# Attention of two heads at a time on the two halves of the PE array, with other PSUM banks

## The chip, the cores and the metric

One core of a Trainium2 chip runs the whole kernel. The metric is the device time of one execution in microseconds (us). Engines: PE is TensorE (matmuls), DVE is VectorE, ACT is ScalarE, POOL is GpSimd, SP issues the DMAs.

## What is computed

The reference runs one sequence of 256 tokens, 1024 features, in float32 through two blocks. The first block has two layers, each a mixer and a gated feed-forward with a short convolution. Each mixer has two attentions of 8 heads with 64 channels a head, so there are four attentions, which this case is about:

- even mixer, second half: chunked attention with a bias by relative position (relb);
- even mixer, first half: attention to 64 keys a query, chosen by index scores (4 index heads, relu, weighted sum, the 64 largest);
- odd mixer, second half: window attention of 8 query heads on 2 key heads, with a sink in the softmax;
- odd mixer, first half: causal attention with forget gates added to the logits.

```python
logits = einsum('bqhd,bshd->bhqs', q, k) * dh ** -0.5   # plus bias, mask, gates or sink
p = softmax(logits); out = einsum('bhqs,bshd->bqhd', p, v)
y = concatenate([first half, second half]); h = h + y @ w_out
```

The second block (a gated delta rule, a long convolution, a feed-forward, a gate) follows; the change does not touch it.

## The kernel before

Everything stays on the chip as [features, tokens] or [tokens, features] tiles; the weights (some 190 MB in pieces of 1 MB) are read once, in order, by SP. Matmuls with weights run in three products of parts: each piece is split into two parts `hi` (ScalarE, line 208) and `lo` (VectorE, line 209), each input `xs` likewise. Matmuls of the attention run in plain float32, which the profile shows as two passes each. A planner orders each engine's instructions before the run, by priority in the order of the program and by its own costs; on the chip each engine works through its own fixed queue. So PE's queue holds matmuls of projections (`mmA`, `mmB`) and of the output projection (`mmO`) between the steps of the softmax.

`attend` (lines 522 to 550) does one head. `at_s` are the logits in one PSUM bank of tag s: queries 0:128 against keys 0:128, queries 128:256 against keys 0:256, with 64 rows of the array (64 channels), head 0 of a pair on partitions 0 to 63, head 1 on 64 to 127. `logits` adds the mask or bias on VectorE into `at_l`; two reductions give minus the maxima `at_nm`; ScalarE takes exps into `at_p` with the sums `at_sm`; VectorE takes reciprocals and multiplies. Three transposes go into `at_t` (one bank, tag tr), ScalarE copies them to `at_pT`, and `at_y` (two matmuls with 64 columns of the array, so 64 partitions of the output) sums over keys. `attention` (552 to 560) runs eight heads, two in one bank of tag y, which is then split into `xs1` (lines 296 and 297).

PSUM has 8 banks. In a mixer (line 638) mm has 4, s 2, tr 1, y 1; the tag t of small products is put on s (line 642). `out_proj` (562 to 578) asks for four mm banks at once (`ac`), each for two feature tiles; its first two weight pieces belong to the half of the heads that came first and need no output of the attention in progress, the other two do; `residual` (line 372) adds each bank to `h`, and the feed-forward `ffn` starts from that `h` (its products are `mmU`). The weights' parts have two buffers each of `hi` and `lo` and one more from the phase's own pool (lines 162 to 173), taken in turn.

`to_feat` (596) transposes through bank s; the index scores (721 to 732), `fk` (845 to 850), `rel_logits` (743), `mask_logits` (615) and `forget_logits` (859) go head by head; `rel_logits` loads each head's bias into its own tile `relb`.

Of the kernel before, what the change touches and what calls it, by code (L numbers as in the profile page):

```python
# [19 lines left out]
T = 256  # L20
D = 1024
# [30 lines left out]
def weight_spec():  # L52
    """Pieces of the weight matrices (matrix, first k tile, k tiles, first column, columns), in order of use."""
# [42 lines left out]
def constants():  # L96
# [23 lines left out]
    # one level of a doubling: identity minus the lower (upper) left blocks, within 64 positions  # L120
# [31 lines left out]
class Weights:  # L152
    """Weight pieces in order: loaded whole, and split into two parts that add up to them exactly."""
# [60 lines left out]
def emit(ctx, tc, A):  # L214
# [7 lines left out]
    def phase(stack, name, tags):  # L222
        """PSUM banks of a phase: tag -> number."""
# [25 lines left out]
    # an early use of the scalar engine: its table is there when the data come  # L249
# [15 lines left out]
    def mmA(out, w, xs, m, k0=0, start=True, stop=True, ks=None):  # L265
        """out [128 features, T] += the piece's m-th 128 columns against xs, both in two parts."""
# [9 lines left out]
    def mmN(out, raw, x, m):  # L276
        """the same in float32."""
# [4 lines left out]
    def mmB(out, w, xs, j, c0=0, cn=None):  # L282
        """out [128 tokens of half j, columns] = xs^T against the piece."""
# [8 lines left out]
    def split_into(xs_k, src, scale=None):  # L292
        """xs_k [128, (k tiles,) 2T] = the two parts of src (times scale)."""
# [22 lines left out]
    def rsqrt(out, m, n):  # L316
        """out = 1/sqrt(m) of a small tile, by Newton's steps; few columns each on their own."""
# [16 lines left out]
    def square_acc(k, src, dst, **scale):  # L334
        """dst [128, T] = running sum over k of src's squares."""
# [8 lines left out]
    def mean_cols(*parts):  # L344
        """sums over features / D of [128, T] tiles, as columns [128 tokens, 2] in PSUM."""
# [6 lines left out]
    def row_bcast(col, name, ps=None):  # L352
        """columns [128 tokens, 2] -> [128, T] in PSUM, the same row on every partition."""
# [18 lines left out]
    def residual(i, ps):  # L372
        """h += ps [128, 2, T], two feature tiles; acc = the running sum of h's squares."""
# [14 lines left out]
    def pieces_A(name, xs, n, use, parts=None):  # L388
        """n pieces of a matrix with 8 k tiles; use(i, psum [128, 2, T])."""
# [14 lines left out]
    def ffn(up, dn, g, conv, beside=None):  # L404
        with ExitStack() as st:
# [5 lines left out]
            def scale(dst, ps):  # L411
                """dst = ps times the tokens' factors, two channel tiles."""
# [3 lines left out]
            # without a convolution the factors come after the product; else only the first pairs go ahead of them  # L416
# [77 lines left out]
    def pick_rows(p):  # L494
        """[128, 8] bf16: column n picks the rows n of the three parts of running sums."""
# [6 lines left out]
    def thrice(p, src, n, tag="thrice"):  # L502
        """[128, n, 128] of [128, n, 8]: three copies for the three parts' rows, zero elsewhere."""
# [6 lines left out]
    def three_parts(g, p, ps, tag="rest"):  # L510
        """g = bf16 parts of [128, w] in PSUM that add up to it: the first in rows 0:64, the others in 64:96 and 96:128."""
# [8 lines left out]
    QB = ((0, 128), (128, 384))  # columns of the two query blocks: keys 0:128, keys 0:256  # L520

    def attend(hd, qT, kT, v, logits, ap, y, sink):
        """One head: qT, kT [64, T]; v(kb) [128, 64]; y [64, T] in PSUM."""
        ps = bank("s", "at_s")
        mm(ps[:, 0:128], qT[:, 0:128], kT[:, 0:128])
        mm(ps[:, 128:384], qT[:, 128:256], kT)
        L = logits(hd, ps)
        nm = small(2, "at_nm", 3)
        for j, (a, b) in enumerate(QB):
            V.tensor_reduce(nm[:, j:j + 1], L[:, a:b], AX.X, OP.max, negate=True)  # L530
        if sink is not None:
            V.tensor_scalar(nm, nm, sink[1][:, hd:hd + 1], None, OP.min)
        pr = ap.tile([128, 384], F32, tag="at_p", name="at_p", bufs=3)
        sm = small(2, "at_sm", 3)
        for j, (a, b) in enumerate(QB):
            S.activation(pr[:, a:b], L[:, a:b], AF.Exp, bias=nm[:, j:j + 1], accum_out=sm[:, j:j + 1])
        if sink is not None:
            es = small(2, "at_es", 3)
            S.activation(es, nm, AF.Exp, bias=sink[0][:, hd:hd + 1])
            V.tensor_tensor(sm, sm, es, OP.add)  # L540
        V.reciprocal(sm, sm)
        for j, (a, b) in enumerate(QB):
            V.tensor_scalar(pr[:, a:b], pr[:, a:b], sm[:, j:j + 1], None, OP.mult)
        tp = bank("tr", "at_t")
        for b in range(3):
            transpose(tp[:, 128 * b:128 * b + 128], pr[:, 128 * b:128 * b + 128])
        pT = ap.tile([128, 384], F32, tag="at_pT", name="at_pT", bufs=3)
        S.copy(pT, tp[:, :384])
        mm(y, v(0), pT[:, 0:256], True, False)
        mm(y[:, 128:256], v(1), pT[:, 256:384], False, True)  # L550

    def attention(qT, kT, vN, logits, ap, ys, k0, kv=lambda hd: hd, sink=None):
        """Eight heads; qT: [128, pairs, T] (head hd on partitions 64*(hd%2)), vN [128, 2, 64*heads]."""
        for p in range(4):
            yp = bank("y", "at_y")
            for hd in (2 * p, 2 * p + 1):
                o, c = 64 * (hd % 2), kv(hd)
                attend(hd, qT[o:o + 64, p], kT(hd, o), lambda kb: vN[:, kb, 64 * c:64 * c + 64], logits, ap,
                       yp[o:o + 64, :T], sink)
            split_into(ys[:, k0 + p], yp[:, :T])  # L560

    def out_proj(name, ys, first):
        """h += ys against a matrix; the half of the k tiles from `first` on comes first."""
# [16 lines left out]
    def rope(dst, src, nh, ap):  # L580
        """src, dst [128, 2, nh*64]."""
# [14 lines left out]
    def to_feat(dst, src, n):  # L596
        """src [128 tokens, 2, n*128] -> dst [128, n, T]."""
        for a in range(0, n, 2):
            ps = bank("s", "tf")
# [6 lines left out]
    def nat(name, xs, *parts):  # L606
        """A piece by the stationary tokens; parts: (destination [128, 2, ..], its column, piece's column, n, scale)."""
# [7 lines left out]
    def mask_logits(m, ap):  # L615
        def f(hd, ps):
            t = ap.tile([128, 384], F32, tag="at_l", name="at_l", bufs=3)
            V.tensor_tensor(t, ps[:, :384], m, OP.add)
            return t
        return f  # L620

    def log1pexp(dst, x, n):
        """dst = log(1 + exp(-|x|)), by the series of atanh."""
# [14 lines left out]
    ATT = {"mm": 4, "s": 2, "tr": 1, "y": 1}  # L638

    def att_phase(st, name):  # L640
        phase(st, name, ATT)
        banks["t"] = banks["s"]

# [1 line left out]
    with ExitStack() as st:  # L645
# [6 lines left out]
        # index keys and weights, index queries: in float32  # L652
# [9 lines left out]
        # the tensor engine's clock rises with work: it starts before the data come  # L662
        warm = bank("s", "warm")
# [30 lines left out]
        # layer norm of the index keys  # L694
# [852 lines left out]
```

## Time and profile before

| | |
|---|---|
| time, median of 3 runs | 1282.49 us (1282.23 to 1282.65) |
| span of the profiled execution | 1280.9 us, first to last instruction |
| mean granted TensorE clock in it | 0.990 |
| PE, DVE, ACT, POOL busy | 98%, 76%, 56%, 1% |
| four attentions, by PE's first at_s to last at_y | 62.7 to 91, 118.4 to 144, 375.7 to 404, 426.9 to 453 us |

The profile gives no time for the profiled execution other than its span; the median of the runs is 1.6 us above it. Busy time of PE counts a matmul from its start to its modelled end, and matmuls overlap, so what a matmul costs in a stream is read from start to start. A form such as 64*128 is rows times columns of the array in use.

### The profile page before, as it was taken

Reading aid. Unit: us, or ns where it says so; the run is one execution under the profiler, and the core shown is the slowest. Engines: PE = TensorE matmul, PEld = TensorE weight load, DVE = VectorE, ACT = ScalarE, POOL = GpSimd, SP = SyncE. Lnnn points to the kernel's source line nnn. Section 1 sums busy time; section 2 is a strip of 40 time slices with the busy share of each in tenths; the row PEclk is TensorE's granted clock in tenths of the full one; section 3 lists DMA queues with packets and bytes.
Section 4 is the critical chain, followed back from the end, with each engine's and each line's share of the span. In section 5 each row is a group of like instructions: output and inputs, shape, how many; then the busy total and the mean of one; then the engine's idle time right before and its main releaser. Section 6 shows DMA issues by size and latency. Waiting matters only on the chain.

```text
span 1280.9 us, 25239 instructions
## 1 busy us (share of the span) xinstructions
PE 1252.6 (98%) x10452; PEld 1192.3 (93%) x10452; DVE 976.9 (76%) x2024; ACT 717.7 (56%) x1204; POOL 11.6 (1%) x21
## 2 busy tenths in 40 slices
PE   8999999999999999999999999999999999999997
PEld 8978899999988889999988998889899999999997
DVE  6976698785497679878549888889997778666546
ACT  4465566664365556565425379888643654444433
POOL 0000000000000000000010000000000000000000
PEclk8999999999999999999999999999999999999999
DMA  6543355555342255554514332212234556555542
GB/s 228 181 153 132 132 180 186 195 179 187 135 165 88 78 198 182 184 195 170 193 64 177 133 132 100 100 35 78 88 133 147 182 193 205 190 194 189 181 154 86
DMA packets 29923, 195.45 MB, mean 153 GB/s; under 512 B 3568, under 2 KB 5104, under 8 KB 9712
## 3 DMA queue, kind: packets, MB, share of 16 engines
q1 hardware_dynamic: 29808, 193.83, 42.8%
q8 instruction: 82, 1.34, 0.4%
q14 instruction: 33, 0.27, 0.1%
HBM read 192.77 MB, written 1.05 MB: 151 GB/s over the span
## 4 chain that ended last, share of the span: by engine, by line
PE 74%; issue 11%; ACT 3%; DVE 3%; POOL 1%; ACTq 0%; POOLq 0%; DVEq 0%
PE mmU L260 29%; PE mmD L260 15%; PE mmA L260 12%; PE mmB L260 4%; PE mmO L260 3%; PE mmF L260 2%; PE at_y L260 2%; PE at_s L260 1%; PE sr L260 1%; ACT hi L208 1%; PE do L260 1%; PE at_t L263 1%; DVE lo L209 1%; PE mc L260 0%; ACT xbd L1150 0%
## 5 line engine op out<-in xcount | busy, mean ns | idle before, releaser
L208 ACT CAST hi<-raw 128x1024 fp32r<-128x1024 f32 (+2 forms) x273 | 336.3, 1252 | 322.4 <-PE mmU L260 138.6
L209 DVE TENSOR_TENSOR lo<-raw,hi 128x1024 fp32r<-128x1024 f32 (+2 forms) x273 | 400.1, 1476 | 134.5 <-ACT hi L208 133.9
L260 PE MATMUL mmU<-xs,hi 128*128 128x256 f32 x2112 | 373.6, 280 | 3.8 <-DVE h L385 3.8
L260 PEld LDWEIGHTS mmU<-xs,hi 128*128 128x128 f32 x2112 | 323.5, 188 | 4.4 <-ACT xs L299 3.2
L260 PE MATMUL mmU<-xs,lo 128*128 128x256 f32 x1056 | 296.4, 281 | 1.8 <-DVE lo L209 1.8
L260 PE MATMUL mmA<-xs,hi 128*128 128x256 f32 x1152 | 224.9, 291 | 0.2 <-ACT hi L208 0.2
L260 PEld LDWEIGHTS mmU<-xs,lo 128*128 128x128 f32 x1056 | 198.6, 188 | 2.5 <-DVE lo L209 2.4
L260 PE MATMUL mmD<-hid,hi 128*128 128x256 f32 x1056 | 190.2, 283 | 0.0
L260 PEld LDWEIGHTS mmA<-xs,hi 128*128 128x128 f32 x1152 | 181.8, 191 | 2.8 <-issue 1.5
L260 PE MATMUL mmA<-xs,lo 128*128 128x256 f32 x576 | 166.1, 289 | 1.3 <-DVE lo L209 1.2
L260 PEld LDWEIGHTS mmD<-hid,hi 128*128 128x128 f32 x1056 | 164.7, 192 | 0.0
L260 PE MATMUL mmD<-hid,lo 128*128 128x256 f32 x528 | 149.4, 283 | 0.0
L260 PEld LDWEIGHTS mmA<-xs,lo 128*128 128x128 f32 x576 | 110.0, 191 | 2.8 <-DVE lo L209 1.7
L1274 DVE SCALAR_TENSOR_TENSOR cv<-cpad,par,cv 128x256 f32<-128x256 f32 x240 | 107.6, 478 | 0.5
L260 PEld LDWEIGHTS mmD<-hid,lo 128*128 128x128 f32 x528 | 101.4, 192 | 0.0
L260 PE MATMUL mmB<-hi,xs 128*128 128x256 f32 x416 | 77.8, 285 | 0.9 <-DVE h L385 0.9
L260 PEld LDWEIGHTS mmB<-hi,xs 128*128 128x128 f32 x416 | 64.8, 190 | 2.2 <-issue 1.8
L260 PE MATMUL mmA<-hg,raw 128*128 128x256 f32 x256 | 65.1, 391 | 0.9 <-PE mmD L260 0.9
L452 DVE SCALAR_TENSOR_TENSOR cv<-mmU,par,cv 128x255 f32<-128x255 f32 (+1 forms) x144 | 60.9, 474 | 1.6 <-ACT cv L450 1.3
L260 PE MATMUL mmB<-lo,xs 128*128 128x256 f32 x208 | 59.4, 285 | 0.0
L260 PEld LDWEIGHTS mmA<-hg,raw 128*128 128x128 f32 x256 | 46.5, 193 | 6.3 <-PE mmD L260 1.1
L260 PE MATMUL mmO<-xs,hi 128*128 128x256 f32 x256 | 49.5, 288 | 0.0
(448 smaller groups left out, 1765.5 us busy)
## 6 DMA issues: line engine op xcount, KB each, us to landing
raw<-in_wts_dram SPq DMA_DIRECT2D x157, 1024.0 KB, 4.8
raw<-in_wts_dram SPq DMA_DIRECT2D x24, 896.0 KB, 4.5
relb<-in_relb_dram SPq DMA_DIRECT2D x8, 192.0 KB, 4.1
h<-in_xT_dram SPq DMA_DIRECT2D x4, 256.0 KB, 3.9
out_dram<-xg SPq DMA_DIRECT2D x2, 512.0 KB, 2.6
cst<-in_cst_dram SPq DMA_DIRECT2D x1, 640.0 KB, 8.8
buf<-in_g_plp_dram SPq DMA_DIRECT2D x1, 512.0 KB, 5.0
gfin<-in_g_fin_dram SPq DMA_DIRECT2D x1, 512.0 KB, 5.2
```

The lines of the kernel that those rows point to most:

```text
L208: self.nc.scalar.copy(hi[:, a:b], r[:, a:b])
L209: self.nc.vector.tensor_tensor(lo[:, a:b], r[:, a:b], hi[:, a:b].bitcast(F32), OP.subtract)
L260: PE.matmul(out, lhsT=lhsT, rhs=rhs, start=start, stop=stop, skip_group_check=True)
L263: PE.transpose(out, in_, ident)
L452: V.scalar_tensor_tensor(y[:, d:], x[:, :T - d], cw[:, 3 * ch + 2 - d:3 * ch + 3 - d], y[:, d:], OP.mult, OP.add)
L1274: V.scalar_tensor_tensor(cv[:, k], cpad[:, k, t:t + T], cw[:, t:t + 1], cv[:, k], OP.mult, OP.add)
```

## The change

Two heads take each step together. `attend` is gone; `attention` runs four times, once a pair. The logits of both heads go into one tile of two banks (`bank2`), the head on rows 0 to 63 and the head on rows 64 to 127 in turn, one bank each. Add, maxima, products and copy are single instructions for both heads; the exps stay one a head and query block. The probabilities stay in the logits' tile `at_l`. The products with v go in turn to the two column halves, which are two halves of the partitions of the same bank. The sink's exp takes one instruction for both heads and blocks, with an add ahead of it. PSUM is shared as mm 3, s 2, tr 2, y 1, so that s and tr hold one pair each, and t is put on y. Index scores, `fk`, masks, biases and forget gates go by pairs; `to_feat` uses s and tr in turn; the biases by relative position are loaded straight into `at_l`. `out_proj` is as it was. Comments are dropped.

```diff
+    def bank2(tag, name):
+        p, tag, n = banks[tag]
+        return p.tile([128, 2, 512], F32, tag=tag, name=name, bufs=n // 2)
...
     def attention(qT, kT, vN, logits, ap, ys, k0, kv=lambda hd: hd, sink=None):
+        two = (slice(0, 64), slice(64, 128))
         for p in range(4):
+            heads = (2 * p, 2 * p + 1)
+            ps = bank2("s", "at_s")
+            for first in (True, False):
+                for m, hd in enumerate(heads):
+                    q, k = qT[two[m], p], kT(hd, 64 * m)
+                    if first:
+                        mm(ps[:, m, 0:128], q[:, 0:128], k[:, 0:128])
+                    else:
+                        mm(ps[:, m, 128:384], q[:, 128:256], k)
+            L = logits(p, ps[:, :, :384])
+            nm, sm = small(4, "at_nm", 3), small(4, "at_sm", 3)
+            for j, (a, b) in enumerate(QB):
+                V.tensor_reduce(nm[:, 2 * j:2 * j + 2], L[:, :, a:b], AX.X, OP.max, negate=True)
...
+            pr = L
+            for m in range(2):
+                for j, (a, b) in enumerate(QB):
+                    c = slice(2 * j + m, 2 * j + m + 1)
+                    S.activation(pr[:, m, a:b], pr[:, m, a:b], AF.Exp, bias=nm[:, c], accum_out=sm[:, c])
+            if sink is not None:
+                es = small(4, "at_es", 3)
+                V.tensor_tensor(by_j(es), by_j(nm), both(sink[0]), OP.add)
+                S.activation(es, es, AF.Exp)
+                V.tensor_tensor(sm, sm, es, OP.add)
+            V.reciprocal(sm, sm)
+            for j, (a, b) in enumerate(QB):
+                V.tensor_tensor(pr[:, :, a:b], pr[:, :, a:b], sm[:, 2 * j:2 * j + 2].to_broadcast([128, 2, b - a]),
+                                OP.mult)
+            tp = bank2("tr", "at_t")
+            for m in range(2):
+                for b in range(3):
+                    transpose(tp[:, m, 128 * b:128 * b + 128], pr[:, m, 128 * b:128 * b + 128])
+            pT = ap.tile([128, 2, 384], F32, tag="at_pT", name="at_pT", bufs=2)
+            S.copy(pT, tp[:, :, :384])
             yp = bank("y", "at_y")
+            for kb in range(2):
+                for m, hd in enumerate(heads):
+                    c = 64 * kv(hd)
+                    mm(yp[two[m], 128 * kb:T], vN[:, kb, c:c + 64], pT[:, m, 256 * kb:256 + 128 * kb], kb == 0, kb == 1)
             split_into(ys[:, k0 + p], yp[:, :T])
...
     def to_feat(dst, src, n):
         for a in range(0, n, 2):
-            ps = bank("s", "tf")
+            ps = bank2("s" if a % 4 else "tr", "tf")[:, 0]
...
-            t = ap.tile([128, 384], F32, tag="at_l", name="at_l", bufs=3)
-            V.tensor_tensor(t, ps[:, :384], m, OP.add)
+            t = ap.tile([128, 2, 384], F32, tag="at_l", name="at_l", bufs=3)
+            V.tensor_tensor(t, ps, m[:, None, :].to_broadcast([128, 2, 384]), OP.add)
...
-    ATT = {"mm": 4, "s": 2, "tr": 1, "y": 1}
+    ATT = {"mm": 3, "s": 2, "tr": 2, "y": 1}
...
         phase(st, name, ATT)
-        banks["t"] = banks["s"]
+        banks["t"] = banks["y"]
...
-            rb_ = ap.tile([128, 384], F32, tag="relb", name="relb", bufs=2)
-            nc.sync.dma_start(rb_, A["relb"][:, hd])
-            V.tensor_tensor(t, ps[:, :384], rb_, OP.add)
+            nc.sync.dma_start(t, A["relb"][:, pair(p)])
+            V.tensor_tensor(t, ps, t, OP.add)
...
+            for m in range(2):
+                hd = 2 * p + m
+                for j, (a, b) in enumerate(QB):
+                    V.scalar_tensor_tensor(t[:, m, a:b], ps[:, m, a:b], fq[:, 8 * j + hd:8 * j + hd + 1], fk[:, hd, a:b],
+                                           OP.add, OP.add)
```

## Rows read from the trace of the kernel before

**Rows 1.** The page: span, PE's busy time, PE's weight loads for mmU.
```profile
span 1280.9 us, 25239 instructions
...
PE 1252.6 (98%) x10452; PEld 1192.3 (93%) x10452; DVE 976.9 (76%) x2024; ACT 717.7 (56%) x1204; POOL 11.6 (1%) x21
...
L260 PEld LDWEIGHTS mmU<-xs,hi 128*128 128x128 f32 x2112 | 323.5, 188 | 4.4 <-ACT xs L299 3.2
```
**Rows 2.** Windows of four attentions: length; busy us of PE, PEld, DVE, ACT, POOL; clock.
```profile
62.40:91.50 29.10, 27.80 (x175) 20.64 (x174) 21.61 (x60) 18.05 (x52) 0.00 (x0) 1.00 0.40 147
118.30:144.50 26.20, 25.62 (x168) 19.09 (x167) 18.55 (x56) 17.02 (x49) 0.00 (x0) 1.00 0.25 88
375.50:404.30 28.80, 28.59 (x187) 21.89 (x187) 22.40 (x89) 18.10 (x58) 0.00 (x0) 1.00 0.22 79
426.90:453.70 26.80, 26.49 (x168) 19.77 (x168) 19.78 (x63) 16.91 (x49) 0.00 (x0) 1.00 0.21 78
```
**Rows 3.** Timeline of PE in the second attention: start, length, work, matmuls.
```profile
118.36 0.93 PE L260 MATMUL at_s<-kaT,qaT 64*128 64x128 f32 x8
119.22 0.39 PE L260 MATMUL mmO<-xs,hi 128*128 128x256 f32 x1
...
123.62 0.28 PE L260 MATMUL mmO<-xs,hi 128*128 128x256 f32 x1
123.82 0.92 PE L260 MATMUL at_s<-kaT,qaT 64*128 64x128 f32 x4
124.67 0.86 PE L260 MATMUL at_y<-at_pT,va 128*64 128x256 f32 x4
125.47 0.55 PE L263 MATMUL at_t<-cst,at_p 128*128 128x128 f32 x3
125.77 0.36 PE L260 MATMUL mmO<-xs,hi 128*128 128x256 f32 x1
```
**Rows 4.** Chain of waits in order of time: start, us, what.
```profile
169.82 116.63 PE mmU L260 x988
```
**Rows 5.** Timeline of PE: first and last visit of at_s and of at_y.
```profile
62.73 0.93 PE L260 MATMUL at_s<-kbT,qbT 64*128 64x128 f32 x8
...
70.90 0.86 PE L260 MATMUL at_y<-at_pT,vb 128*64 128x256 f32 x4
...
441.68 0.70 PE L260 MATMUL at_s<-kcT,qcT 64*128 64x256 f32 x2
...
452.42 0.86 PE L260 MATMUL at_y<-at_pT,vc 128*64 128x256 f32 x4
```
**Rows 6.** VectorE's instructions by form, 62 to 454 us: count, busy us, mean ns.
```profile
L530 DVE TENSOR_REDUCE at_nm<-at_l 128x1 f32<-128x256 f32 x32 | 13.1, 409 | 0.0
L543 DVE TENSOR_SCALAR at_p<-at_p,at_sm 128x256 f32<-128x256 f32 x32 | 11.1, 347 | 0.0
L543 DVE TENSOR_SCALAR at_p<-at_p,at_sm 128x128 f32<-128x128 f32 x32 | 8.9, 279 | 0.1
...
L461 DVE TENSOR_TENSOR hid<-sil,hid 128x512 fp32r<-128x512 f32 x11 | 7.5, 685 | 0.1
...
L297 DVE TENSOR_TENSOR xs<-at_y,xs 128x256 fp32r<-128x256 f32 x16 | 6.8, 424 | 17.7 <-ACT xs L296 17.7
```
**Rows 7.** ScalarE's instructions by form, 90 to 144 us.
```profile
L548 ACT COPY at_pT<-at_t 128x384 f32<-128x384 f32 x9 | 4.3, 476 | 3.5 <-PE at_t L263 3.4
L536 ACT ACTIVATE at_p<-at_l,at_nm 128x256 f32<-128x256 f32 x8 | 4.0, 504 | 0.4 <-DVE at_nm L530 0.4
...
L604 ACT COPY qaT<-tf 128x512 f32<-128x512 f32 x2 | 1.1, 590 | 0.7 <-PE tf L263 0.7
```
**Rows 8.** Timeline of ScalarE after the second attention's last at_y.
```profile
146.76 1.91 ACT L208 CAST hi<-raw 128x2048 fp32r<-128x2048 f32 x1 [2.75 <-PE mmO L260]
```
**Rows 9.** Timeline of VectorE, same place.
```profile
148.70 2.29 DVE L209 TENSOR_TENSOR lo<-raw,hi 128x2048 fp32r<-128x2048 f32 x1 [4.23 <-ACT hi L208]
```
**Rows 10.** Timeline of PE where the feed-forward begins.
```profile
159.58 0.48 PE L260 MATMUL mmU<-xs,hi 128*128 128x256 f32 x2 [1.39 <-DVE h L385]
```
**Rows 11.** The page: DMA issues.
```profile
relb<-in_relb_dram SPq DMA_DIRECT2D x8, 192.0 KB, 4.1
```

More of the change, by code (lines that the diff above doesn't have):

```diff
@@ L520, in emit @@
     QB = ((0, 128), (128, 384))
[L522 to L550, printed above, removed]
@@ L552, in attention @@
     def attention(qT, kT, vN, logits, ap, ys, k0, kv=lambda hd: hd, sink=None):
+        two = (slice(0, 64), slice(64, 128))
         for p in range(4):
+            heads = (2 * p, 2 * p + 1)
[11 more added lines that the diff above has]
+                V.tensor_reduce(nm[:, 2 * j:2 * j + 2], L[:, :, a:b], AX.X, OP.max, negate=True)
+            by_j = lambda t: t.rearrange("p (j m) -> p j m", j=2)
+            both = lambda t: t[:, None, 2 * p:2 * p + 2].to_broadcast([128, 2, 2])
+            if sink is not None:
+                V.tensor_tensor(by_j(nm), by_j(nm), both(sink[1]), OP.min)
+            pr = L
[3 more added lines that the diff above has]
+                    S.activation(pr[:, m, a:b], pr[:, m, a:b], AF.Exp, bias=nm[:, c], accum_out=sm[:, c])
+            if sink is not None:
+                es = small(4, "at_es", 3)
[12 more added lines that the diff above has]
+            S.copy(pT, tp[:, :, :384])
@@ L555, in attention @@
             yp = bank("y", "at_y")
[L556 to L559, printed above, removed]
+            for kb in range(2):
+                for m, hd in enumerate(heads):
+                    c = 64 * kv(hd)
+                    mm(yp[two[m], 128 * kb:T], vN[:, kb, c:c + 64], pT[:, m, 256 * kb:256 + 128 * kb], kb == 0, kb == 1)
@@ L615, in mask_logits, with f @@
     def mask_logits(m, ap):
-        def f(hd, ps):
-            t = ap.tile([128, 384], F32, tag="at_l", name="at_l", bufs=3)
-            V.tensor_tensor(t, ps[:, :384], m, OP.add)
+        def f(p, ps):
+            t = ap.tile([128, 2, 384], F32, tag="at_l", name="at_l", bufs=3)
+            V.tensor_tensor(t, ps, m[:, None, :].to_broadcast([128, 2, 384]), OP.add)
             return t
@@ L661, in emit @@
                 V.tensor_scalar(hg[:, k], h[:, k], g, None, OP.mult)
-        warm = bank("s", "warm")
+        warm = bank("y", "warm")
         for _ in range(WARM):
@@ L720, in emit @@
         so = ap.tile([128, 384], F32, name="so")
-        for hd in range(4):
-            o, p = 64 * (hd % 2), hd // 2
-            ps = bank("s", "ix")
-            mm(ps[:, 0:128], qiT[o:o + 64, p, 0:128], kiT[o:o + 64, 0, 0:128])
-            mm(ps[:, 128:384], qiT[o:o + 64, p, 128:256], kiT[o:o + 64, 0])
-            rl = ap.tile([128, 384], F32, tag="rl", name="rl", bufs=2)
-            S.activation(rl, ps[:, :384], AF.Relu)
-            for j, (a, b) in enumerate(QB):
-                if hd == 0:
-                    V.tensor_scalar(so[:, a:b], rl[:, a:b], wi[:, j, hd:hd + 1], None, OP.mult)
-                else:
-                    V.scalar_tensor_tensor(so[:, a:b], rl[:, a:b], wi[:, j, hd:hd + 1], so[:, a:b], OP.mult, OP.add)
+        for p in range(2):
+            ps = bank2("tr" if p else "s", "ix")
+            for first in (True, False):
+                for m in range(2):
+                    q, k = qiT[64 * m:64 * m + 64, p], kiT[64 * m:64 * m + 64, 0]
+                    if first:
+                        mm(ps[:, m, 0:128], q[:, 0:128], k[:, 0:128])
+                    else:
+                        mm(ps[:, m, 128:384], q[:, 128:256], k)
+            rl = ap.tile([128, 2, 384], F32, tag="rl", name="rl", bufs=1)
+            S.activation(rl, ps[:, :, :384], AF.Relu)
+            for m in range(2):
+                hd = 2 * p + m
+                for j, (a, b) in enumerate(QB):
+                    if hd == 0:
+                        V.tensor_scalar(so[:, a:b], rl[:, m, a:b], wi[:, j, hd:hd + 1], None, OP.mult)
+                    else:
+                        V.scalar_tensor_tensor(so[:, a:b], rl[:, m, a:b], wi[:, j, hd:hd + 1], so[:, a:b], OP.mult,
+                                               OP.add)
         V.tensor_tensor(sc, sc, so, OP.add)
@@ L741, in emit, with rel_logits @@
             nat("even_in", xs0, (vb, 256 * i, 0, 256, r))
-        def rel_logits(hd, ps):
-            t = ap.tile([128, 384], F32, tag="at_l", name="at_l", bufs=3)
-            rb_ = ap.tile([128, 384], F32, tag="relb", name="relb", bufs=2)
-            nc.sync.dma_start(rb_, A["relb"][:, hd])
-            V.tensor_tensor(t, ps[:, :384], rb_, OP.add)
+        def rel_logits(p, ps):
+            t = ap.tile([128, 2, 384], F32, tag="at_l", name="at_l", bufs=3)
+            nc.sync.dma_start(t, A["relb"][:, pair(p)])
+            V.tensor_tensor(t, ps, t, OP.add)
             return t
@@ L828, in emit @@
         V.tensor_tensor(lf, fx, lf, OP.subtract)
-        ps = bank("s", "fq")
+        ps = bank("y", "fq")
         mm(ps[:, 0:8], C["le"], lf[:, 0:8])
@@ L838, in emit @@
         l3 = thrice(ap, lf.rearrange("p (j n) -> p j n", j=2), 2)
-        ps = bank("s", "fs")
+        ps = bank2("s", "fs")[:, 0]
         mm(ps[:, :T], l3[:, 0], leo, True, False)
@@ L844, in emit @@
         fk = ap.tile([128, 8, 384], F32, name="fk")
-        for hd in range(8):
-            ps = bank("s", "fk")
-            mm(ps[:, :T], pick[:, hd:hd + 1].to_broadcast([128, 128]), fsum)
-            V.tensor_tensor(fk[:, hd, 0:128], C["mcaus"], ps[:, :128], OP.subtract)
-            S.activation(fk[:, hd, 128:256], ps[:, :128], AF.Copy, scale=-1.0)
-            V.tensor_tensor(fk[:, hd, 256:384], C["mcaus"], ps[:, 128:T], OP.subtract)
+        mc2 = C["mcaus"][:, None, :].to_broadcast([128, 2, 128])
+        for p in range(4):
+            ps = bank2("s" if p % 2 else "tr", "fk")
+            for m in range(2):
+                hd = 2 * p + m
+                mm(ps[:, m, :T], pick[:, hd:hd + 1].to_broadcast([128, 128]), fsum)
+            V.tensor_tensor(fk[:, pair(p), 0:128], mc2, ps[:, :, :128], OP.subtract)
+            S.activation(fk[:, pair(p), 128:256], ps[:, :, :128], AF.Copy, scale=-1.0)
+            V.tensor_tensor(fk[:, pair(p), 256:384], mc2, ps[:, :, 128:T], OP.subtract)
         qcT = ap.tile([128, 4, T], F32, name="qcT")
@@ L857, in emit, with forget_logits @@
             nat("odd_in", xs0, (vc, 256 * i, 0, 256, r))
-        def forget_logits(hd, ps):
-            t = ap.tile([128, 384], F32, tag="at_l", name="at_l", bufs=3)
-            for j, (a, b) in enumerate(QB):
-                V.scalar_tensor_tensor(t[:, a:b], ps[:, a:b], fq[:, 8 * j + hd:8 * j + hd + 1], fk[:, hd, a:b],
-                                       OP.add, OP.add)
+        def forget_logits(p, ps):
+            t = ap.tile([128, 2, 384], F32, tag="at_l", name="at_l", bufs=3)
+            for m in range(2):
+                hd = 2 * p + m
+                for j, (a, b) in enumerate(QB):
+                    V.scalar_tensor_tensor(t[:, m, a:b], ps[:, m, a:b], fq[:, 8 * j + hd:8 * j + hd + 1], fk[:, hd, a:b],
+                                           OP.add, OP.add)
             return t
```

## The prediction

> **What bounds the kernel now.** I read the page first: PE is busy for 98% of the span [rows 1]. So nothing saves time that doesn't shorten PE's queue, unless it ends one of PE's few waits. Then the windows of the four attentions, the only stretches in which the change does other work: PE is busy for 27.80 of 29.10, 25.62 of 26.20, 28.59 of 28.80 and 26.49 of 26.80 us at clock 1.00, VectorE for 71 to 78%, ScalarE for 62 to 65% [rows 2]. PE is never short of work there because the scheduler has laid projection or output matmuls (mmB, mmA, mmO: "filler") between the steps of the softmax. Then PE's timeline inside one attention, to price what PE does [rows 3], and the chain of waits for the price of filler in an undisturbed stream: 116.63 us for 988 matmuls, 0.118 us each [rows 4].
>
> In [rows 3] the reader is to see one thing above all. At 118.36 a line holds eight at_s matmuls, which are two heads (two matmuls a head, each shown as two passes), and mmO follows 0.86 us later. At 123.82 a line holds four, one head, and the next work follows after 0.85 us. Two heads on the two row halves (64*128) cost what one costs. It came about where the scheduler happened to put two heads side by side; after 118.36 it mostly didn't.
>
> **The price of a visit.** I call an unbroken run of at_s or at_y on PE a visit. An at_s visit lasts 0.85 us with one head and 0.86 with two; an at_y visit lasts 0.80 (124.67 to 125.47). Entering costs more: from the last filler at 123.62 to at_s at 123.82 are 0.20 us, where filler follows filler in 0.118, so 0.08 for the entry (the exit lies inside the 0.85). Counted in the timeline over the four attentions there are 28 visits of at_s (6 with two heads, 18 with one, and 2 heads broken into two visits each) and 32 of at_y, one a head; first and last of each kind in [rows 5].
>
> **The change part by part, on PE.**
> (1) at_s by pairs, 16 visits of two heads. Before: 6 x 0.86 + 18 x 0.85 + 2 x 0.95 = 22.4, and 28 entries x 0.08 = 2.2; after 16 x (0.86 + 0.08) = 15.0. Saved: 9.6 us. Both prices are seen.
> (2) at_y by pairs, 16 visits; the heads share all 128 rows and take the two column halves (128*64) in turn. Before 32 x 0.88 = 28.2. No row of the trace shows two column halves of one set of rows at once, so bounds. If they overlap as the row halves do: 16 x (0.81 + 0.08) = 14.2, saved 14.0. If they don't overlap, 16 x (1.60 + 0.08) = 26.9, saved 1.3; and if each turn from half to half also costs an exit and an entry (0.16, the exit put like the entry), 64 of these (four runs in each visit) in place of 32 make it 5.1 slower. I take 14.0: the nearest row is at_s at 118.36, the same float32 form on the other kind of half.
> The Trainium skill speaks against that in TensorE: Matmul & The Clock Gate, Part 3, The mechanism: a weight load overlaps matmuls in flight only where its row group differs, and the two heads of at_y have the same rows. The trace bears it out badly in that wording: mmU's loads of 188 ns on all rows [rows 1] lie beside matmuls that start every 0.118 us [rows 4]. By the rule part (2) would save 1.3, and the time would be that of the first rival.
> (3) Six transposes a pair as before; no change on PE.
>
> **What moves off PE.** VectorE: TENSOR_TENSOR costs 0.424 us for 256 columns and 0.685 for 512, so 1.02 ns a column [rows 6]. Per pair, one add of 768 columns about 0.95 where two of 384 stood (0.424 + 128 x 1.02 ns = 0.55 each); reductions of 256 and 512 columns 0.41 + 0.68 (1.06 ns a column more) for 2 x (0.27 + 0.41); products of 256 and 512 columns 0.42 + 0.69 for 2 x (0.28 + 0.35); one reciprocal less. That is 3.3 for 4.0 us a pair. The fourth attention keeps its four adds a pair (scalar operands). ScalarE: exps as before; one copy of 768 columns: 0.476 for 384 and 0.590 for 512 give 0.89 ns a column, about 0.82, for 2 x 0.48 [rows 7]. None of it is on the end-setting path, but the cover shrinks. With each window shorter by 5.9 us (23.6 / 4), VectorE would be busy for 18.55 - 2.8 = 15.8 of 20.3 us (78%) in the second attention and some 17.5 of 20.9 (84%) in the fourth [rows 2]. PE would then catch up with softmax steps that aren't ready. The windows of before leave PE idle for 0.2 to 1.3 us each; I put 1.0 us more a window, 4 in all. Lower bound 0; upper bound 2.7 a window, the tail of a pair from its transposes to the split of y (0.65 + 0.82 + 0.37 + 0.42, and 0.4 put for hops between engines), should no filler stand there.
>
> **PSUM and the weights' buffers.** mm goes from 4 banks to 3, but out_proj still asks for four accumulators. The fourth can start only when residual(0) has released the first, that is after the last at_y: 48 of out_proj's 192 matmuls move behind it. PE isn't left idle by that: of a window of 20.3 us (26.2 - 5.9) visits take 7.3 (29.2 / 4) and 24 transposes 2.4 (three take 0.30, 125.47 to 125.77 in [rows 3]); the other 10.6 us are 90 matmuls, and 126 can go ahead of the last at_y. 66 (7.8 us) come after it at least, 48 of them the fourth accumulator's. Behind the waiting matmuls stands something else: the output matrix' second piece keeps its hi/lo buffers until the fourth accumulator has used them, and the first piece of the feed-forward needs these. Today its hi waits 2.75 us for mmO at 146.76 [rows 8] and its lo is done at 151 [rows 9], well ahead of mmU at 159.58, which itself waits 1.39 us for the residual [rows 10]. After the change that hi (1.9) and lo (2.3) run at the very end, beside the residuals; between 1.8 us lost a layer (4.2 us of splitting against 24 matmuls or 2.8 us of cover, and 0.4 of queueing) and 1.4 won (if mmU's first bank is no longer the last accumulator's). I take 0.5 lost, 1 for both layers.
>
> **Edits at nothing.** Index scores by pairs, fk by pairs, the sink's exp on both heads, to_feat in turn on s and tr: VectorE and ScalarE work of 0.1 to 0.5 us each, covered by PE's queue, which is full beside them; at most 0.5 in all if that cover is gone. Bank t is now y's single bank in place of the two of s: the norms' few steps are a chain one after another anyhow. The relb loads, 8 of 192 KB, become 4 of 384 KB into at_l itself; 192 KB take 4.1 us to land [rows 11]. Pair 3's load waits on SP's queue for pair 0's buffer, with weight loads behind it; pair 0's transposes are done some 8 us into the attention and pair 3's add isn't due before 14, so nothing is late.
>
> **The sum** against the profiled execution: -9.6 - 14.0 + 4 + 1 = -18.6. Its span is 1280.9 us; the median of the runs is 1282.49, 1.6 us more (what lies around the span stays). Forecast 1282.5 - 18.6 = 1263.9, said as 1264. Without the two losses it is 1258.9; with the upper bounds of both (10.8 and 3.6), 1273.3.
>
> **Rivals.**
> Column halves don't overlap: -9.6 - 1.3 + 1, and with less pressure 2 of new idle time: 1274.6 (with turns that cost: 1281). For it: no row shows the overlap. Against: the row halves do it in the same form.
> Everything keeps up: no new idle time and mmU starts no later, 1258.9. For it: VectorE would still be under 85%. Against: the order on PE is fixed before the run, so any late step stalls filler behind it.
> Slower: a pair's chain becomes the bound. s, tr and y each hold one pair only. A pair's chain is 0.86 at_s, 0.95 add, 1.09 reductions, 2.0 exps on ScalarE (four, 0.50 each at most), 0.16 + 1.1 reciprocal and products, 0.9 transposes, 0.82 copy, 0.81 at_y, 0.8 split, with hops some 10 us. If pairs don't overlap at all, an out_proj attention takes 10 + 3 x 10, and 8.3 for the 66 matmuls and the drain, 48.3 us, where now from 118.36 to where mmU begins to wait (159.58 - 1.39) there are 39.8. Two of these cost +17.0; the other two attentions have filler to spare and still win 11.8: +5.2, 1288. It decides above a cycle of about 9 us a pair. Against it: at_l has three buffers, and the next at_s needs no more than the add of the pair before, so two pairs are in work at any time and the cycle is nearer to VectorE's 3.3 + 0.4 us plus the weights' splitting.
> No change: the same with a cycle within some 0.4 us of that 9.
>
> **How the numbers follow.** Forecast (1260 to 1272) 0.58; everything keeps up 0.12; no overlap of column halves 0.18; no change 0.06; slower 0.06. The range from 1257.5 to 1276.5 takes in the first two and most of the third. A measurement here can tell about 0.2%, 2.6 us. Faster than 1279.9: 0.58 + 0.12 + nearly all of 0.18, 0.86; within 0.2%: 0.08; slower: 0.06.
>
> **What would show it.** In the changed trace: at_s lines of eight passes in about 0.86 us, 16 of them; at_y lines of eight in about 0.81 (1.6 is the first rival); four windows of 20 to 22 us, with PE's idle time under 2 us in each (much more: the chain); mmU's first wait after each out_proj no longer than 1.4 + 1.8 us. The forecast is wrong if at_y pairs take 1.6, if the windows keep their length while PE's idle time grows, or if the stretches between the attentions get longer by what the attentions lose.

## The result, and the profile after

The changed kernel takes 1264.4 us (median of 4 runs, 1263.16 to 1266.62) where the kernel before takes 1282.36 us beside it: 0.9862 of it, 95% interval 0.9845 to 0.9879. The forecast was 1264.0 us. The span of the profiled execution went from 1280.9 to 1261.4 us, by 19.5.

The page of the changed kernel, the rows that answer to [rows 1]: span; busy time, share and instructions of each engine; PE's weight loads for `mmU`.

```profile
span 1261.4 us, 25071 instructions
...
PE 1229.7 (97%) x10452; PEld 1179.9 (94%) x10452; DVE 974.5 (77%) x1920; ACT 712.3 (56%) x1178; POOL 11.6 (1%) x21
...
L265 PEld LDWEIGHTS mmU<-xs,hi 128*128 128x128 f32 x2112 | 323.8, 188 | 5.2 <-issue 3.1
```

PE has as many matmuls as before (10452) and is busy 22.9 us less; VectorE and ScalarE lost 104 and 26 instructions and only 2.4 and 5.4 us. So the gain is PE's, as argued, and the question is which of its visits gave it. The windows of the four attentions, from the first `at_s` to the split after the last `at_y`, columns as in [rows 2]:

```profile
62.00:85.90 23.90, 22.52 (x180) 18.13 (x179) 20.19 (x36) 17.11 (x48) 0.00 (x0) 1.00 0.40 152
111.80:133.40 21.60, 21.25 (x171) 16.95 (x170) 17.44 (x31) 15.66 (x45) 0.00 (x0) 1.00 0.27 97
364.30:389.60 25.30, 24.35 (x197) 20.06 (x197) 24.30 (x63) 17.90 (x53) 0.00 (x0) 1.00 0.24 86
411.60:437.90 26.30, 24.88 (x199) 20.46 (x198) 19.12 (x44) 15.77 (x45) 0.00 (x0) 1.00 0.31 117
```

PE's idle time is 1.38, 0.35, 0.95 and 1.42 us (1.30, 0.58, 0.21 and 0.31 in [rows 2]). The timeline of PE in the first of them (start, length, engine, line, work, count of passes, idle time before and its releaser) shows what the visits became:

```profile
62.06 0.93 PE L265 MATMUL at_s<-kbT,qbT 64*128 64x128 f32 x8
62.91 0.38 PE L265 MATMUL mmB<-hi,xs 128*128 128x256 f32 x1
63.13 0.28 PE L265 MATMUL mmB<-lo,xs 128*128 128x256 f32 x1
63.25 0.40 PE L265 MATMUL mmB<-hi,xs 128*128 128x256 f32 x2
...
68.22 0.93 PE L265 MATMUL at_s<-kbT,qbT 64*128 64x128 f32 x8 [1.02 <-DVE at_l L770]
...
70.17 0.30 PE L268 MATMUL at_t<-cst,at_l 128*128 128x128 f32 x1 [0.35 <-DVE at_l L563]
...
71.27 0.37 PE L265 MATMUL mmB<-hi,xs 128*128 128x256 f32 x1
71.47 0.28 PE L265 MATMUL mmB<-lo,xs 128*128 128x256 f32 x1
...
72.39 0.49 PE L265 MATMUL at_s<-kbT,qbT 64*128 64x128 f32 x4
72.82 0.87 PE L265 MATMUL at_y<-at_pT,vb 128*64 128x256 f32 x8
73.62 0.70 PE L265 MATMUL at_s<-kbT,qbT 64*128 64x256 f32 x2
74.25 0.33 PE L268 MATMUL at_t<-cst,at_l 128*128 128x128 f32 x1
74.50 0.70 PE L265 MATMUL at_s<-kbT,qbT 64*128 64x256 f32 x2
75.13 0.76 PE L268 MATMUL at_t<-cst,at_l 128*128 128x128 f32 x5
```

Two things are to be seen. Eight passes of `at_y`, two heads, leave PE after 0.80 us (72.82 to 73.62): the column halves overlap, and the trace has the passes start two by two, 0.007 us apart. And the last pair's `at_s` is broken into three visits, 0.43, 0.63 and 0.63 us, with `at_y` and a transpose between; a whole pair (62.06 to 62.91) takes 0.85. Five of the 16 pairs are broken like that, so `at_s` has 23 visits.

To see where the 19.5 us lie, PE's time was split by what it did, from each instruction's start to the next one's, idle time apart, over the two stretches that hold the attentions: from the first `mmA` to the first `mmU` of layer one, and from the last `mmD` of layer one to the first `mmU` of layer two ("the mixers" from here on).

| us on PE in the mixers | before | after | change |
|---|---|---|---|
| `at_s` | 23.05 | 17.26 | -5.8 |
| `at_y` | 25.43 | 12.89 | -12.5 |
| `mmA`, `mmB`, `mmO` | 179.64 | 176.15 | -3.5 |
| transposes `at_t` | 9.06 | 9.37 | +0.3 |
| small products, the rest | 9.90 | 10.03 | +0.1 |
| idle | 6.59 | 9.61 | +3.0 |
| all | 253.67 | 235.31 | -18.4 |

The remaining -1.1 is outside: the feed-forwards -0.5 and +0.7, start and end +0.3, and -1.7 in the delta rule, which the change doesn't touch (see the run of the banks).

### The profile page after: what moved, and what is told of

Same layout as the page of the kernel before. It is cut to its first block, busy times and chain, and to the rows that moved or that the text cites. A ratio compares the mean times of both kernels' runs of the same rounds, so it can differ in the third digit from the quotient of the medians.

```text
span 1261.4 us, 25071 instructions
## 1 busy us (share of the span) xinstructions
PE 1229.7 (97%) x10452; PEld 1179.9 (94%) x10452; DVE 974.5 (77%) x1920; ACT 712.3 (56%) x1178; POOL 11.6 (1%) x21
## 4 chain that ended last, share of the span: by engine, by line
PE 74%; issue 11%; DVE 4%; ACT 3%; POOL 1%; POOLq 0%; ACTq 0%; DVEq 0%
PE mmU L265 29%; PE mmD L265 15%; PE mmA L265 12%; PE mmB L265 3%; PE mmO L265 3%; PE mmF L265 2%; DVE lo L209 1%; PE sr L265 1%; ACT hi L208 1%; PE do L265 1%; PE at_y L265 1%; PE at_t L268 1%; PE at_s L265 1%; PE mc L265 0%; PE mmP L265 0%
## 5 line engine op out<-in xcount | busy, mean ns | idle before, releaser
L457 DVE SCALAR_TENSOR_TENSOR cv<-mmU,par,cv 128x255 f32<-128x255 f32 (+1 forms) x144 | 65.1, 478 | 11.4 <-ACT cv L455 10.3
L455 ACT ACTIVATE cv<-mmU,par 128x256 f32<-128x256 f32 x72 | 38.6, 558 | 20.0 <-DVE cv L457 20.0
```

The source lines that it names most:

```text
L455: S.activation(y, x, AF.Identity, bias=cb[:, ch:ch + 1], scale=cw[:, 3 * ch + 2:3 * ch + 3])
L457: V.scalar_tensor_tensor(y[:, d:], x[:, :T - d], cw[:, 3 * ch + 2 - d:3 * ch + 3 - d], y[:, d:], OP.mult, OP.add)
```

## The experiments

**Do the row halves carry the gain of `at_s`?** Both heads take the channels of the first head, so both sit on rows 0 to 63.

```diff
-                    q, k = qT[two[m], p], kT(hd, 64 * m)
+                    q, k = qT[two[0], p], kT(heads[0], 0)
```

> The changed kernel, but both logits of a pair are taken from the first head's channels, on rows 0 to 63 of the array (so the second head's attention is computed from the first head's queries and keys); nothing else moves. Theory (PE bounds; two heads on two row halves cost one visit): at_s runs of eight passes grow from 0.86 to about 1.62 us, 13 whole pairs and parts of the rest, +10.5 us, 1275 us, windows of the attentions 2.6 us longer each. Rival (the gain came from fewer VectorE and ScalarE instructions and fewer visits, not from the overlap): at most +3 us, 1267 us.

Measured: 1266.77 us, ratio 0.9882 (0.9853 to 0.9912). PE's timeline in the first attention:

```profile
62.09 1.57 PE L265 MATMUL at_s<-kbT,qbT 64*128 64x128 f32 x8
63.59 0.38 PE L265 MATMUL mmB<-hi,xs 128*128 128x256 f32 x1
```

By its time alone this run fits the rival (at most 1267) and not the theory (1275), so the trace has to decide. The pair takes 1.50 us where it took 0.85: on the same rows nothing overlaps. In the mixers `at_s` costs 25.43 instead of 17.26 us, 8.2 more, but the mixers get only 4.8 us longer, because 2.6 us of idle time are gone (9.61 to 7.06; the waits of 1.02 and 0.35 us seen above at 68.22 and 70.17 are not there) and the projections take 0.6 less. Another 1.7 us went outside the mixers, in the first feed-forward (0.9) and the delta rule (0.8). So the mechanism stands, and its price was overstated: where PE waits for VectorE a little later, a longer visit partly fills that wait.

**Do the column halves carry the gain of `at_y`?** Copy and products go head by head again.

```diff
-            tp = bank2("tr", "at_t")
-            for m in range(2):
+            tp, yp = bank2("tr", "at_t"), bank("y", "at_y")
+            for m, hd in enumerate(heads):
                 for b in range(3):
                     transpose(tp[:, m, 128 * b:128 * b + 128], pr[:, m, 128 * b:128 * b + 128])
...
-            S.copy(pT, tp[:, :, :384])
+                S.copy(pT, tp[:, m, :384])
```

> The changed kernel, but transposes, copy and the product with v are done head by head, so that at_y is 32 visits of one head again. Theory (PE bounds, the column halves overlap): 16 visits of 0.88 us more, 14.1 us, less 1 to 2 us of idle time of PE that the fuller queue hides: +12.5, 1277 us. Rival (at_y's pairs gain only what the merged copies gain): at most +3 us, 1267 us.

Measured: 1279.46 us, 0.9973 (0.9955 to 0.9991); the span is 13.8 us above the changed kernel's. PE in the first attention:

```profile
71.95 0.86 PE L265 MATMUL at_y<-at_pT,vb 128*64 128x256 f32 x4
72.74 0.55 PE L268 MATMUL at_t<-cst,at_l 128*128 128x128 f32 x3
73.22 0.93 PE L265 MATMUL at_s<-kbT,qbT 64*128 64x128 f32 x8
74.08 0.86 PE L265 MATMUL at_y<-at_pT,vb 128*64 128x256 f32 x4
```

One head alone holds PE for 0.79 us, two together for 0.80. In the mixers `at_y` goes from 12.89 back to 25.40 us, the projections take 1.4, transposes 1.4 and idle time 1.0 more, while `at_s` takes 2.8 less, since here only two of the 16 pairs are broken; 13.6 in sum. The rival's 1267 us is excluded, and the pairs of `at_y` are most of the change's gain.

**Does it need the heads in turn?** The pair's matmuls go head 0, head 0, head 1, head 1.

```diff
-            for first in (True, False):
-                for m, hd in enumerate(heads):
+            for m, hd in enumerate(heads):
+                for first in (True, False):
...
-            for kb in range(2):
-                for m, hd in enumerate(heads):
+            for m, hd in enumerate(heads):
+                for kb in range(2):
```

> The changed kernel with the matmuls of the two heads not in turn: all of the first head's, then all of the second's, for the logits and for the products with v. Theory (PE lets the second head's matmuls start beside the first's wherever both stand next in its queue, as at 118.36 us of the kernel before, where the queue held one head after the other): no change, 1264.4 us within 2. Rival (the turn-taking makes the overlap): at_s +10 and at_y +12.5, up to 1287 us; if it is needed for the column halves alone, 1277 us.

Measured: 1265.61 us, 0.9872 (0.9843 to 0.9901), the same as the changed kernel within the intervals. PE's timeline:

```profile
73.97 0.92 PE L265 MATMUL at_s<-kbT,qbT 64*128 64x128 f32 x4
74.82 0.88 PE L265 MATMUL at_y<-at_pT,vb 128*64 128x256 f32 x8
75.63 0.49 PE L265 MATMUL at_s<-kbT,qbT 64*128 64x128 f32 x2
```

`at_y` by heads still takes 0.81 us, so the order inside a pair is free: it is enough that both heads stand next to each other. The order shows only where a pair is broken: the line at 73.97 holds two matmuls of one head and lasts 0.85 us; in the changed kernel the line at 72.39 holds one of each head, 0.43.

**Do the merged VectorE instructions matter?** Add, maxima and products go head by head, PE's work stays.

```diff
-                V.tensor_reduce(nm[:, 2 * j:2 * j + 2], L[:, :, a:b], AX.X, OP.max, negate=True)
+                V.tensor_reduce(nm[:, 2 * j + m:2 * j + m + 1], L[:, m, a:b], AX.X, OP.max, negate=True)
...
-                V.tensor_tensor(pr[:, :, a:b], pr[:, :, a:b], sm[:, 2 * j:2 * j + 2].to_broadcast([128, 2, b - a]),
-                                OP.mult)
+                    V.tensor_scalar(pr[:, m, a:b], pr[:, m, a:b], sm[:, 2 * j + m:2 * j + m + 1], None, OP.mult)
...
-            V.tensor_tensor(t, ps, m[:, None, :].to_broadcast([128, 2, 384]), OP.add)
+            for n in range(2):
+                V.tensor_tensor(t[:, n], ps[:, n], m, OP.add)
```

> The changed kernel, but VectorE's adds, reductions and products are single instructions of one head again (as in the kernel before); PE's and ScalarE's work is that of the changed kernel. Theory (PE bounds, VectorE is covered): some 2.8 us more VectorE work an attention, of which 0 to 0.8 us shows: +1.5, 1266 us. Rival (the chain of the pair on VectorE is what got shorter): all of it shows, +8 to +11 us, 1273 to 1275 us.

Measured: 1269.53 us, 0.99 (0.9864 to 0.9935). That is 5.1 us more than the changed kernel, between the theory's 1.5 and the rival's 8 to 11. The mean granted clock is 0.987 or 0.988 in all four runs, and 0.988 to 0.991 in those of the changed kernel. In the profile the span is 7.6 us longer, 4.9 of it outside the mixers, mostly before the first `mmA` (2.4) and in the delta rule (2.5). The mixers are 2.7 us longer than the changed kernel's, all of it (3.3) in the first of them and -0.6 in the second. Windows of the first attention of this run (columns as above):

```profile
70.00:74.00 4.00, 2.16 (x13) 1.38 (x13) 3.45 (x13) 3.15 (x13) 0.00 (x0) 1.00 0.02 6
74.20:77.80 3.60, 3.60 (x17) 2.16 (x16) 1.71 (x3) 1.50 (x5) 0.00 (x0) 0.53 0.63 184
```

and the same stretches of the changed kernel:

```profile
70.00:74.00 4.00, 3.83 (x32) 3.20 (x32) 3.93 (x9) 3.35 (x14) 0.00 (x0) 1.00 0.87 319
74.20:77.80 3.60, 3.60 (x27) 2.64 (x27) 2.78 (x7) 2.71 (x7) 0.00 (x0) 1.00 0.08 27
```

PE waits in the first stretch (busy for 2.16 of 4.00 us), and right after that the granted clock is 0.53, about the lower of its two levels, 1.2 GHz, for 3.4 us. At half speed that stretch does 1.7 us less work, which is over half of the 3.3. Without it the mixers are 1.0 us longer, near the 1.5 of the forecast; the whole time is not, and how much of it belongs to the separate instructions isn't shown. A wait followed by the lower clock is seen once more below; that the one causes the other isn't shown by these runs.

**What do the banks do alone?** The kernel before with the changed kernel's shares.

```diff
-    ATT = {"mm": 4, "s": 2, "tr": 1, "y": 1}
+    ATT = {"mm": 3, "s": 2, "tr": 2, "y": 1}
```

> The kernel before, head by head, with nothing changed but PSUM's shares: mm 3, s 2, tr 2, y 1 in place of 4, 2, 1, 1. Theory (the fourth accumulator of out_proj and the feed-forward's first weight piece come later, nothing else bounds): 0.5 us lost a layer, +1 (between -2.8 and +3.6), 1283 us, with some 48 matmuls of mmO more behind the last at_y. Rival (a second bank for the transposes is what sped the softmax up): 5 us or more faster, 1277 us.

Measured: 1280.25 us, 0.9994 (0.998 to 1.0008): no difference clear of the interval, so the rival's 5 us are excluded. In its profile the mixers take 253.72 us where the kernel before takes 253.67. The expected 48 matmuls don't show: 128 and 117 of `mmO` stand behind the last `at_y` in the two layers, where the kernel before has 122 and 117. What the third bank does shows at the feed-forwards: in this run the first `mmU` waits longer (1.74 us in layer two),

```profile
159.22 0.47 PE L260 MATMUL mmU<-xs,hi 128*128 128x256 f32 x2 [1.73 <-DVE h L385]
```

and a wait that the kernel before has a little later, for `lo`, is gone in both layers:

```profile
162.95 0.39 PE L260 MATMUL mmU<-xs,lo 128*128 128x256 f32 x1 [0.63 <-DVE lo L209]
```

Each feed-forward, from its first `mmU` on, takes 188.53 us in place of 189.95. So head by head the three banks cost 0.3 us a layer at `mmU` and win 1.4 behind it.

The span is 3.8 us shorter than the kernel before's: 2.8 in these feed-forwards and 2.2 in the delta rule, far from the banks, against 1.2 more before the first `mmA`. The windows bear on the delta rule: the kernel before, this run, and the changed kernel around the place where they differ (PE's granted clock is the third number from the end).

```profile
728.00:744.00 16.00, 16.00 (x93) 14.97 (x92) 12.22 (x44) 7.62 (x12) 0.00 (x0) 0.79 0.18 62
```

```profile
728.00:744.00 16.00, 16.00 (x112) 14.96 (x112) 13.22 (x49) 7.60 (x13) 0.00 (x0) 1.00 0.24 92
```

```profile
712.00:725.00 13.00, 13.00 (x77) 12.15 (x78) 10.33 (x39) 6.05 (x10) 0.00 (x0) 0.87 0.08 16
```

At 1.2 GHz for part of each stretch, 0.79 and 0.87 mean about 6.7 us of it in the first (16 x 0.21 / 0.5) and 3.4 in the third (13 x 0.13 / 0.5); the second has none. At half speed that is 3.4, 1.7 and 0 us of work lost. Between the kernel before and the changed one this is 1.7, as much as the delta rule got shorter; for the banks' run it would be 3.4 where 2.2 were measured, so it doesn't account for every tenth. The code there is the same in all three kernels, and what moves these stretches isn't shown; it is a reason to compare the mixers and not whole spans.

**What would whole pairs of `at_s` give?** The four logits' matmuls of a pair get priority in the planner.

```diff
+            with tc.high_priority():
                 for first in (True, False):
                     for m, hd in enumerate(heads):
```

> The changed kernel with the four logits matmuls of a pair put ahead of all else that is ready in the planner, so that every pair's at_s is one visit: 16 visits where the changed kernel has 23, 13.8 us where it has 17.25, and 7 entries of 0.08 less. Theory now (PE bounds only in part, as the run with both heads on the same rows showed: of 8.15 us more at_s 4.8 came through in the attentions): of 4.0 us 2.4 come through, 1262 us. Rival one (PE bounds wholly): 4.0 us, 1260.4. Rival two (the softmax steps bound): 0, 1264.4.

Measured: 1258.2 us (1255.87 to 1260.31), 0.9815 (0.9798 to 0.9832): faster than the theory's 1262; rival one's 1260.4 lies within the interval. PE in the first attention:

```profile
59.94 0.93 PE L265 MATMUL at_s<-kbT,qbT 64*128 64x128 f32 x8
60.80 0.50 PE L265 MATMUL mmB<-hi,xs 128*128 128x256 f32 x2
...
71.61 0.87 PE L265 MATMUL at_y<-at_pT,vb 128*64 128x256 f32 x8
72.41 0.88 PE L268 MATMUL at_t<-cst,at_l 128*128 128x128 f32 x6
...
78.73 0.87 PE L265 MATMUL at_y<-at_pT,vb 128*64 128x256 f32 x8 [0.85 <-DVE xs L302]
```

The first line is the fourth pair's `at_s`, whole, 10 us ahead of the first transposes (69.90); 16 visits, 13.70 us in place of 17.26. The mixers take 231.59 us, 3.7 less than the changed kernel's: 3.6 from `at_s`, and 0.6 less idle time against 0.4 more for projections and transposes. A new wait stands at 78.73, where `at_y` waits for the single bank y, but it is no longer than the one at 68.22 that went. So here all of what `at_s` saved came through, as rival one had it, and not the share that the run on the same rows suggested.

**Is the fourth mm bank worth having back?** mm 4 and tr 1, transposes and copies by head, the four `at_y` matmuls kept together; alone, and with the priority.

```diff
-    ATT = {"mm": 3, "s": 2, "tr": 2, "y": 1}
+    ATT = {"mm": 4, "s": 2, "tr": 1, "y": 1}
...
-            tp = bank2("tr", "at_t")
             for m in range(2):
+                tp = bank("tr", "at_t")
...
+            with tc.issue_after(last.ins):
+                times_v(0, 0)
```

> The changed kernel with mm 4 and tr 1: transposes and copy go head by head through one bank, the product with v stays by pairs (the second head's first in the queue). Theory (three banks cost 0.5 us a layer, and the copies' 0.16 us a head more on ScalarE are covered): -1, 1263.5 us, mmO's tail and mmU's start as in the kernel before. Rival (one bank for the transposes lengthens the chain of a pair, the second head's wait for the first one's copy, some 0.8 us a pair, and the softmax steps bound): +3 to +10 us, 1267 to 1275.

> Both of the last two: the logits of a pair as one visit, and four banks for mm. Theory: the two add up, -2.4 and -1, 1261 us. Rival: what the logits win is lost in the chain through one transpose bank, 1264 us or more.

Measured: 1264.92 us, 0.9876 (0.9856 to 0.9895) alone, and 1260.51 us, 0.9835 (0.9811 to 0.9859) with the priority: neither better than its partner with three banks. The first lies between its theory and its rival, the second at its theory's 1261, with the rival's 1264 at the edge of its interval. PE where the feed-forwards start, in the run without priority, and in the changed kernel:

```profile
154.73 0.47 PE L265 MATMUL mmU<-xs,hi 128*128 128x256 f32 x2 [1.39 <-DVE h L390]
```

```profile
148.53 0.47 PE L265 MATMUL mmU<-xs,hi 128*128 128x256 f32 x2 [1.71 <-DVE h L390]
...
449.87 0.47 PE L265 MATMUL mmU<-xs,hi 128*128 128x256 f32 x2 [1.80 <-DVE h L390]
...
453.14 0.39 PE L265 MATMUL mmU<-xs,lo 128*128 128x256 f32 x1 [1.25 <-DVE lo L209]
```

The wait is 1.39 again, as in [rows 10], so the 0.3 to 0.4 us a layer are the third bank's. The second mixer is 2.1 us shorter with four banks than in the changed kernel; the first is 3.7 longer. There a row of PE's timeline and one of the windows show the same as in the run with separate VectorE instructions, a wait ahead of `at_s` and then the lower clock:

```profile
72.56 0.93 PE L265 MATMUL at_s<-kbT,qbT 64*128 64x128 f32 x8 [1.95 <-DVE at_l L775]
```

```profile
74.20:77.80 3.60, 3.29 (x16) 3.32 (x17) 2.67 (x6) 2.21 (x9) 0.00 (x0) 0.53 0.81 291
```

With the priority neither is there, the mixers take 232.3 us (231.6 with three banks), and the fourth bank's gain at `mmU` is lost elsewhere: PE idles 1.8 us less in the mixers, but the projections take 3.2 more, with the transposes in 36 visits for 20, and each feed-forward takes 0.5 more.

## Why the prediction came out

The mechanism was right: PE bounds the kernel, the gain lies in the visits, both kinds of halves overlap, and the losses are small. That the number was met to 0.4 us is partly luck: `at_s` saved 3.4 us less than put, and 1.7 us less idle time, 1.8 less for the projections and 1.7 less in the delta rule stood against it.

*(1) `at_s` by pairs, -9.6.* This is the term that was mis-sized. Measured are -5.8 in the visits, and five entries fewer at the 0.08 used there, -0.4: -6.2. The price of a pair was right (0.85 for 0.86); what failed is the count, "16 visits of two heads". A pair's four matmuls are four instructions to the planner, and it put other work between them in five pairs, which makes 23 visits. The run with priority, with 16 visits, gets 3.6 us of that back.

*(2) `at_y` by pairs, -14.0.* Measured: -12.5 in the visits, and 16 entries fewer at 0.08, -1.3, so -13.8. The bound taken, that the column halves overlap like the row halves, is shown by the row at 72.82 (0.80 us) and, by the pairs undone, by 12.5 us more. The rule from the Trainium skill (TensorE: Matmul & The Clock Gate, Part 3, The mechanism), by which a weight load overlaps matmuls in flight only across row groups, would, read by itself, have made this 1.3; the trace doesn't agree, since both heads have all 128 rows and cost 0.80 us together.

*(3) Transposes, 0.* +0.3.

*Idle time, +4 in the windows.* +1.7 in the windows; in the mixers +2.3, their +3.0 less the 0.7 at `mmU`. Of that, VectorE's steps (68.22, 70.17 and four more), where the waits were looked for, give 0.6: 2.7 us of waiting for 2.1. Ends of pairs without filler give 1.1, nearly all of it at the last pair of the fourth attention, where PE waits for ScalarE's copy and for the split:

```profile
436.41 0.87 PE L265 MATMUL at_y<-at_pT,vc 128*64 128x256 f32 x8 [0.94 <-ACT at_pT L570]
437.75 0.85 PE L265 MATMUL mmO<-xs,hi 128*128 128x256 f32 x4 [0.47 <-ACT xs L301]
```

VectorE's share of the windows went from between 71 and 78% to between 73 and 96%. The cost of each of its instructions was foreseen, as they show by form (count, busy us, mean ns; 61 to 438 us):

```profile
L563 DVE TENSOR_TENSOR at_l<-at_l,at_sm 128x512 f32<-128x512 f32 x16 | 11.0, 685 | 0.0
L545 DVE TENSOR_REDUCE at_nm<-at_l 128x2 f32<-128x512 f32 x16 | 10.8, 676 | 0.0
L563 DVE TENSOR_TENSOR at_l<-at_l,at_sm 128x256 f32<-128x256 f32 x16 | 6.7, 421 | 0.2
...
L545 DVE TENSOR_REDUCE at_nm<-at_l 128x2 f32<-128x256 f32 x16 | 6.6, 412 | 0.1
L770 DVE TENSOR_TENSOR at_l<-at_s,at_l 128x768 f32<-128x768 f32 x4 | 3.8, 954 | 0.9 <-PE at_s L265 0.6 <-DMA at_l<-in_relb_dram 0.3
```

0.69, 0.68, 0.42, 0.41 and 0.95 us were forecast as 0.69, 0.68, 0.42, 0.41 and 0.95. What did not come is the relief: 0.7 us a pair were put, some 8 in three attentions, and VectorE's busy time fell by 2.4 us over the whole span. Why the waits came out shorter all the same is not shown. That PE catches up less with VectorE when it saves less fits the run on the same rows, 8.2 us more of `at_s` and 2.6 us less idle; but in the run with whole pairs PE saved 3.6 us more and idled 0.6 less.

*Three mm banks and the start of the feed-forward, +1.* +0.7 at `mmU` and +0.2 in the feed-forwards (-0.5 and +0.7). The size was right, and the 0.7 is caused by the bank: the wait is 1.39 to 1.43 us in the profiles with four banks and 1.71 to 1.80 in those with three. The split that comes late was right for layer two alone, where `mmU` waits 1.25 us for `lo` at 453.14; and the banks by themselves won 1.1 us a layer, within the bounds given but with the other sign. The 48 matmuls of the fourth accumulator didn't lengthen the tail: 113 and 84 of `mmO` stand behind the last `at_y`, 122 and 117 before.

*Edits at nothing.* Right as far as seen. The load of 384 KB into `at_l` shows as 0.3 us of VectorE's waiting before four adds, in the last row above; the wait of PE at 68.22 isn't of that kind, since the add ahead of it (67.22 to 68.17) found VectorE without idle time.

*The rest.* The projections took 3.5 us less. 21 visits fewer at 0.08 are 1.7 of it, which the two terms hold. The other 1.8 had no term. The prediction put the exit of a visit inside its 0.85 us, and it isn't there: the first filler behind `at_s` takes 0.22 us (62.91 to 63.13), the next 0.12 (63.13 to 63.25), and the first behind transposes 0.20 (71.27 to 71.47). Of the 1392 projection matmuls in the mixers 166 stood beside other work or a wait before and 136 do after; what these take above the price of an undisturbed one fell from 14.7 to 10.9 us, which is the 3.5 and 0.3 more. With it and the delta rule's -1.7 the sum closes.

*The rivals.* "The column halves don't overlap" (1274.6) and "a pair's chain becomes the bound" (1288) are excluded by the 0.80 us and by windows in which PE idles for at most 1.42. The windows were said to become 20 to 22 us long and are 21.6 to 26.3; that isn't the rival, since the planner put more filler into them (180, 171, 197 and 199 matmuls for 175, 168, 187 and 168), and the `mmO` left after the fourth takes 10.3 us for 14.0. "Everything keeps up" (1258.9) wasn't so here, but the kernel with whole pairs comes to 1258.2.

## What to carry to other kernels

In these runs two matmuls that each leave half of the array idle, by rows or by columns, cost one if they stand next to each other in PE's queue; the order inside the pair matters little, but the planner has to be told to keep the pair together, so look at the number of passes in PE's timeline and count broken pairs. What such pairs save on PE can be read from one place where they happened to meet in the kernel before; to that, add what each visit costs the filler before and behind it, and subtract what PE will wait for the engine behind it. When two profiles are compared, split PE's time by stage and look at the granted clock of each stretch first, since a single stretch at the lower clock is worth as much as a small edit.

## What the runs showed of the hardware

- Two column halves with the same 128 rows overlap fully: 8 passes in 0.80 us, 4 passes in 0.79.
- Two heads on the same 64 rows don't: 1.50 us for 0.85.
- Heads queued one after the other (head 0 twice, head 1 twice) overlap as well as heads in turn, 0.81 us for `at_y`.
- The first projection matmul behind a visit of `at_s` or `at_y` takes 0.22 us, behind transposes 0.20, in the stream 0.12.
- In three kernels the granted clock (the windows above) went to about half (1.2 GHz) at one place of the delta rule for some 6.7, 3.4 or 0 us, where the kernels don't differ. In two others it did so in the first attention, where PE had been busy for 2.16 of 4.00 us in the one and had waited for 1.95 us in the other.
